# RWKV stage: bonus sums behind the next tile's dense products, decayed-key transposes one head pair later

## Chip, cores, metric

One core of one Trainium2 chip runs the whole program as a single launch. The metric is the device time of one execution in microseconds (us). The engines are named as in the profile: PE (TensorE, with PEld for its weight loads), DVE (VectorE), ACT (ScalarE), POOL (GpSimd), SP (SyncE, which here only issues DMAs).

## What is computed

The program is a chain of blocks on a 512x1024 activation: an RWKV-7 time mix with its MLP, a forgetting-attention layer with its MLP, a mixer (gated delta rule in both directions, and latent attention), and an expert-choice MLP. The change lies in the RWKV time mix only. What matters of the reference:

```python
r = xr @ wr
k = xk @ wk
v = xv @ wv
kk = split_heads(k * k_k)
kk = kk / jnp.maximum(jnp.sqrt(jnp.sum(kk * kk, axis=-1, keepdims=True)), L2_EPS)
k = k * (1.0 + (a - 1.0) * k_a)
y = wkv7_scan(rh, split_heads(decay), kh, vh, -kk, kk * ah)
bonus = jnp.sum((rh * kh * r_k), axis=-1, keepdims=True) * vh
```

There are 16 heads of 64 features. The scan over 512 tokens is done in 8 chunks of 64 tokens.

## The kernel before, in words

Activations are kept feature-major: a tile is 128 features (one pair of heads) by 512 tokens, and a 1024-wide tensor is 8 such tiles. The projections r, k and v are dense products in split precision. Each 128x1024 block of weights is loaded by SP (L179), rounded on ACT (`wh`, L181), and its remainder is taken on DVE (`wl`, L183). One output tile is then 24 matmuls on PE (L244 to L246, eight input tiles by three products). Two buffers each hold the raw, high and low weights, so the weights of a tile are made one tile ahead.

The stage of the change is the r projection. `dense_fm` with `use_r` runs over 8 output tiles p. After a tile's matmuls, `make_r` of the tile before runs. PE spreads a head's norm over the tile (`rB`, L303). DVE makes `kkn` from it (L673), then `kp` (L679), the product r·k·r_k (`prod`, L681) and the scan's left operand `ar` (L691 and L692, twice each). POOL makes `kka` (L675) and the right operand `bk` (L693, L694), and ACT makes the exponentials (L666, L668). Then `sum_bonus` (L656) sums `prod` over each head by four small matmuls into one PSUM bank that stays open for the whole stage.

`pairs(0, ...)` is a generator that is advanced by one head pair after each `make_r`, from the third tile on. For one pair it first issues two steps of `spare`, work for a later layer's modulation: each step is one 512 KB tile `mr` (DMA by SP, L328, four buffers) and two matmuls (L342). Then come eight matmuls `bk`x`ar` (L714) into two banks of their own (tag `f`, two buffers). DVE and ACT bring these to SBUF under masks (L723, L734 on DVE; L736 on ACT, then L737 on POOL). ACT or POOL (L746, L741) scales `bk` by the chunk's decay into `dg`, PE transposes `dg` in four pieces (L750), and ACT stores that as `Bh[p]` (L752), which only the scan reads.

After the r projection, `prepare(0)` inverts triangular blocks with a long chain on DVE (L786 to L805) while `pairs(1, ...)` does the second half of the tokens, and then the scan over chunks begins (L910).

Each engine executes its instructions in the order in which the build leaves them. That order is made by a scheduler from the traced program, and `tc.issue_after(x)` ties a traced instruction behind the instruction x on its engine. A wait on a semaphore holds everything that stands behind it on the same engine. Five PSUM banks (tag `b`) serve dense tiles, `rB`, the transposes and the bonus sum. A tile of the r projection is read from its bank until its last L692.

Of the kernel before, what the change touches and what calls it, by code (L numbers as in the profile page):

```python
# [12 lines left out]
AF = mybir.ActivationFunctionType  # L13
# [109 lines left out]
class K:  # L123
# [392 lines left out]
    def rwkv(self, x_dram, G, sh, gt, xT):  # L516
        nc, tc, A = self.nc, self.tc, self.A
# [127 lines left out]
        def use_r(p, pt):  # L645
            held.append((p, pt))
            if p:
                make_r(*held.pop(0))
            if p > 1:
                prep[0].send(None)  # L650

        prods = []

        def sum_bonus(p, prod):
            for tt in range(4):
                nc.tensor.matmul(pbon[:, tt * 16 + 2 * p:tt * 16 + 2 * p + 2], prod[:, tt * 128:tt * 128 + 128],  # L656
                                 self.cst("bo2"), start=(p == 0 and tt == 0), stop=(p == 7 and tt == 3),
                                 skip_group_check=True)

        def make_r(p, pt):  # L660
            rB = spr(p)
            cum, aa = CA[p]
            CA[p] = None
            W = self.wp.tile([128, 8, 65], F32, name=self.nm("W"), tag="w65")
            nc.gpsimd.memset(W[:, :, 0:1], 1.0)
            nc.scalar.activation(W[:, :, 1:65], cum.rearrange("p (c t) -> p c t", t=64), AF.Exp, scale=-C0)  # L666
            Wi = self.s()
            nc.scalar.activation(Wi, cum, AF.Exp, scale=C0)  # L668
            nc.gpsimd.tensor_copy(WCp[:, p, :], W[:, :, 64])
            nc.vector.tensor_copy(WCh[0:64, 2 * p, :], W[0:64, :, 64])  # L670
            nc.vector.tensor_copy(WCh[0:64, 2 * p + 1, :], W[64:128, :, 64])
            kkn = self.s()
            nc.vector.scalar_tensor_tensor(kkn, kT[p], self.col("rw_kk", p), rB, op0=OP.mult, op1=OP.mult)  # L673
            kka = self.s()
            nc.gpsimd.tensor_tensor(kka, kkn, aa, op=OP.mult)  # L675
            t = self.s()
            nc.scalar.activation(t, aa, AF.Identity, scale=self.col("rw_ka", p), bias=oka[:, p:p + 1])
            kp = self.s()
            nc.vector.tensor_tensor(kp, kT[p], t, op=OP.mult)  # L679
            prod = self.s()  # L680
            nc.vector.scalar_tensor_tensor(prod, pt, self.col("rw_rk", p), kp, op0=OP.mult, op1=OP.mult)  # L681
            prods.append((p, prod))
            if p:
                sum_bonus(*prods.pop(0))
            v3 = lambda x, hf: x[:, hf * 256:hf * 256 + 256].rearrange("p (c t) -> p c t", t=64)
            for hf in range(2):
                ar, bk = self.s(), self.s()
                AR[p][hf], BK[p][hf] = ar, bk
                a4, b4 = (z.rearrange("p (c t) -> p c t", t=128) for z in (ar, bk))
                cs = slice(hf * 4, hf * 4 + 4)  # L690
                nc.vector.scalar_tensor_tensor(a4[:, :, 0:64], v3(kkn, hf), -1.0, W[:, cs, 0:64], op0=OP.mult, op1=OP.mult)  # L691
                nc.vector.tensor_tensor(a4[:, :, 64:128], v3(pt, hf), W[:, cs, 1:65], op=OP.mult)  # L692
                nc.gpsimd.tensor_tensor(b4[:, :, 0:64], v3(kka, hf), v3(Wi, hf), op=OP.mult)  # L693
                nc.gpsimd.tensor_tensor(b4[:, :, 64:128], v3(kp, hf), v3(Wi, hf), op=OP.mult)  # L694

        gm = self.cst("gmask")
        idn = self.cst("ident")
        X, BKt, GB = [None, None], [None, None], [None, None]

        def pairs(hf, pool):  # L700

            GBh = GB[hf] = pool.tile([128, 32, 128], F32, name=self.nm("GB"), tag="gb", bufs=1)
            Xh = X[hf] = [None] * 16
            Bh = BKt[hf] = [None] * 8
            for p in range(8):
                g = p // 4
                ar, bk = AR[p][hf], BK[p][hf]
                self.spare(0 if hf else 2)
                pts = [self.bank("f"), self.bank("f")]
                for ci in range(4):  # L710
                    cs = slice(ci * 128, ci * 128 + 128)
                    for hd in range(2):
                        q = slice(hd * 64, hd * 64 + 64)
                        nc.tensor.matmul(pts[hd][:, cs], bk[q, cs], ar[q, cs], start=(ci == 0), stop=(ci == 3),  # L714
                                         skip_group_check=True)
                xo = self.s()
                nc.scalar.activation(xo[0:64], ar[64:128], AF.Copy)
                for hd in range(2):
                    u0 = ((2 * p + hd) % 8) * 4
                    v = pts[hd].rearrange("p (c t) -> p c t", t=128)  # L720
                    o = GBh[g * 64:g * 64 + 64, u0:u0 + 4, :]
                    if hf == 0:
                        nc.vector.tensor_tensor(o, v[0:64], gm[0:64].unsqueeze(1).to_broadcast([64, 4, 128]), op=OP.mult)  # L723
                    else:

                        nc.scalar.activation(o, v[0:64], AF.Copy)
                        nc.gpsimd.memset(o[32:64, :, 0:32], 0.0)
                        nc.gpsimd.tensor_tensor(o[:, :, 64:128], o[:, :, 64:128],
                                                gm[g * 64:g * 64 + 64, 64:128].unsqueeze(1).to_broadcast([64, 4, 64]), op=OP.mult)
                    dst = ar if hd == 0 else xo  # L730
                    d3 = dst[64:128].rearrange("p (c t) -> p c t", t=128)
                    mk = gm[64:128].unsqueeze(1).to_broadcast([64, 4, 128])
                    if hf == 0 and hd == 0:
                        nc.vector.tensor_tensor(d3, v[64:128], mk, op=OP.mult)  # L734
                    else:
                        nc.scalar.activation(d3, v[64:128], AF.Copy)  # L736
                        nc.gpsimd.tensor_tensor(d3, d3, mk, op=OP.mult)  # L737
                Xh[2 * p], Xh[2 * p + 1] = ar, xo
                dg = self.s()
                if hf == 0 and p % 2:  # L740
                    nc.gpsimd.tensor_tensor(dg.rearrange("p (c t) -> p c t", t=128), bk.rearrange("p (c t) -> p c t", t=128),  # L741
                                            WCp[:, p, hf * 4:hf * 4 + 4].unsqueeze(2).to_broadcast([128, 4, 128]), op=OP.mult)
                else:
                    for ci in range(4):
                        cs = slice(ci * 128, ci * 128 + 128)
                        nc.scalar.activation(dg[:, cs], bk[:, cs], AF.Copy, scale=WCp[:, p, hf * 4 + ci:hf * 4 + ci + 1])  # L746
                pt = self.ps()
                for ci in range(4):
                    cs = slice(ci * 128, ci * 128 + 128)
                    nc.tensor.transpose(pt[:, cs], dg[:, cs], idn)  # L750
                Bh[p] = self.s()
                nc.scalar.activation(Bh[p], pt, AF.Copy)  # L752
                yield

        prep = [pairs(0, gb0)]
        self.dense_fm(A["rw_wr"], xr, 0, D, use_r)
        make_r(*held.pop(0))
        prep[0].send(None)
        sum_bonus(*prods.pop(0))
# [6 lines left out]
        with tc.tile_pool(name="rwb", bufs=2, side="right", reuse_waits="tile") as bp:  # L766
# [116 lines left out]
            with self.behind(100000, slots=False):  # L883
                self.run(pairs(1, bp))
                next(pr1)
# [6 lines left out]
            for c in range(8):  # L892
                hf, ci = c // 4, c % 4
# [45 lines left out]
                mid = self.last_pe()  # L939
# [1483 lines left out]
```

## Time and profile before

| what | value |
|---|---|
| device time, three runs | 3038.48 us median (3029.11 to 3039.60) |
| profiled execution, its own time | 3032.97 us |
| span of the profiled execution | 3031.2 us |
| PE busy | 2777.4 us, 92% of the span |
| DVE, ACT, POOL busy | 1619.0, 1049.7 and 727.1 us |
| DMA | 502 MB, 166 GB/s over the span |

The profile's times count from the start of the span. Busy time of an engine is the union of its instructions. PEclk is the clock that TensorE was granted, as a share of full speed: 1.00 is 2.4 GHz, 0.50 is 1.2 GHz. In a timeline a row gives start, length, engine, line, output and inputs, a count, and in brackets the idle time before it with what ended it. A 32-bit matmul of this program can leave more than one record, so a count in the timeline can be a multiple of the number of instructions.

### The profile page before, as it was taken

The page shows a single profiled execution, that of the slowest core. Times are in us where ns is not written, and L with a number is a line of the kernel's source. Part 1 is how long each engine was busy: PE and PEld are TensorE (multiplying, and loading weights), DVE is VectorE, ACT ScalarE, POOL GpSimd, SP SyncE. Part 2 cuts the span into 40 slices and gives each one's busy share as a digit, 9 for nine tenths or more (in the row PEclk, how much of TensorE's full clock was granted, in tenths as well). Part 3 has the DMA queues.
Part 4 walks back from the last instruction along what each step waited for, and adds up shares of the span by engine and source line. Part 5 has one row for each costly group of instructions (what it writes and reads, how often), then busy time and mean ns, then how long its engine had stood idle before and what let it go on. Part 6 is the DMA issues. An engine that isn't in the chain of part 4 may idle for free. (4 is left out here: it accounts for less than half of the span.)

```text
span 3031.2 us, 38070 instructions
## 1 busy us (share of the span) xinstructions
PE 2777.4 (92%) x15046; PEld 1980.8 (65%) x15046; DVE 1619.0 (53%) x2449; ACT 1049.7 (35%) x1703; POOL 727.1 (24%) x563
## 2 busy tenths in 40 slices
PE   6997788999999999999999998898799997999997
PEld 1765466788877777778887776676677884444433
DVE  4565865456674447466645779647765542112112
ACT  2543533422234457442223452253334322110001
POOL 2444553211111034121113453135241121000000
PEclk8997767999999999999999999999999998999999
DMA  6332413346564321446531323242252358899998
GB/s 212 118 95 73 136 55 112 125 153 195 186 219 128 94 81 38 137 159 194 180 98 56 106 74 116 59 132 60 67 175 93 105 188 345 348 378 409 409 409 308
DMA packets 361010, 502.05 MB, mean 166 GB/s; under 512 B 24768, under 2 KB 236992, under 8 KB 360832
## 3 DMA queue, kind: packets, MB, share of 16 engines
q1 hardware_dynamic: 349600, 479.01, 46.5%
q10 hardware_dynamic: 11232, 20.62, 1.8%
q8 instruction: 118, 1.93, 0.3%
q14 instruction: 60, 0.49, 0.0%
HBM read 471.26 MB, written 26.21 MB: 164 GB/s over the span
## 5 line engine op out<-in xcount | busy, mean ns | idle before, releaser
L244 PE MATMUL psb<-s,wh 128*128 128x512 f32 x1384 | 546.1, 395 | 2.9 <-DVE s L977 2.2
L245 PE MATMUL psb<-s,wl 128*128 128x512 f32 x1384 | 543.3, 393 | 0.0
L246 PE MATMUL psb<-s,wh 128*128 128x512 f32 (+1 forms) x1320 | 515.0, 390 | 1.2 <-POOL s L481 0.6
L181 ACT ACTIVATE wh<-wr 128x1024 fp32r<-128x1024 f32 (+1 forms) x221 | 288.2, 1305 | 415.3 <-PE psb L246 266.1
L183 DVE TENSOR_TENSOR wl<-wr,wh 128x1024 fp32r<-128x1024 f32 (+1 forms) x145 | 260.1, 1795 | 261.3 <-ACT wh L181 261.0
L244 PEld LDWEIGHTS psb<-s,wh 128*128 128x128 f32 x1384 | 261.8, 189 | 71.7 <-issue 11.7
L245 PEld LDWEIGHTS psb<-s,wl 128*128 128x128 f32 x1384 | 261.4, 189 | 56.9 <-issue 2.6
L246 PEld LDWEIGHTS psb<-s,wh 128*128 128x128 f32 (+1 forms) x1320 | 247.4, 187 | 58.1 <-issue 2.9
L183 POOL TENSOR_TENSOR wl<-wr,wh 128x1024 fp32r<-128x1024 f32 (+1 forms) x76 | 185.8, 2447 | 397.6 <-ACT wh L181 378.8
L2123 PE MATMUL psb<-rg,s 128*64 128x512 f32 x1024 | 243.0, 598 | 5.3 <-DMA rg<-in_w_up_dram 3.8
L1312 PE MATMUL psf<-f,wh 128*128 128x512 f32 (+1 forms) x688 | 231.5, 410 | 11.0 <-ACT wh L181 10.9
L1008 POOL TENSOR_TENSOR s<-s 128x512 f32<-128x512 f32 x64 | 102.1, 1596 | 514.9 <-ACT s L1006 434.1
L2123 PEld LDWEIGHTS psb<-rg,s 128*64 128x64 f32 x1024 | 83.2, 137 | 142.3 <-issue 120.2
L1312 PEld LDWEIGHTS psf<-f,wh 128*128 128x128 f32 (+1 forms) x688 | 133.0, 194 | 43.1 <-ACT wh L181 12.3
L1312 PE MATMUL psf<-f,wl 128*128 128x512 f32 (+1 forms) x344 | 143.0, 416 | 15.5 <-POOL wl L183 15.4
L2151 PE MATMUL psb<-rg,s 128*64 128x512 f32 (+1 forms) x544 | 129.9, 621 | 0.0
L378 DVE SCALAR_TENSOR_TENSOR mt<-mr,crep,mt 128x512 f32<-128x512 f32 x168 | 126.5, 753 | 3.6
L201 ACT ACTIVATE s<-s 128x512 fp32r<-128x512 f32 x112 | 69.8, 625 | 136.3 <-POOL s L1008 73.1
L1015 DVE SCALAR_TENSOR_TENSOR s<-psb,aff,s 128x512 f32<-128x512 f32 x64 | 45.9, 751 | 129.5 <-PE psb L246 129.5
L1312 PE MATMUL psb<-f,wh 128*128 128x512 f32 (+1 forms) x336 | 107.8, 401 | 7.8 <-DVE f L479 5.9
L2151 PEld LDWEIGHTS psb<-rg,s 128*64 128x64 f32 x544 | 46.2, 148 | 74.2 <-issue 69.4
L1006 ACT ACTIVATE s<-psb 128x512 f32<-128x512 f32 x64 | 37.6, 588 | 164.0 <-PE psb L246 164.0
(565 smaller groups left out, 4946.4 us busy)
## 6 DMA issues: line engine op xcount, KB each, us to landing
rg<-in_w_gate_dram SPq DMA_DIRECT2D x64, 1024.0 KB
rg<-in_w_up_dram SPq DMA_DIRECT2D x64, 1024.0 KB
rg<-in_w_down_dram SPq DMA_DIRECT2D x64, 1024.0 KB
mr<-in_mod_w_dram SPq DMA_DIRECT2D x96, 512.0 KB
wr<-in_mlp_down_dram SPq DMA_DIRECT2D x32, 1024.0 KB
wr<-in_mlp_up_dram SPq DMA_DIRECT2D x31, 1024.0 KB
wr<-in_w_in_dram SPq DMA_DIRECT2D x54, 512.0 KB
mr<-in_w_mod_dram SPq DMA_DIRECT2D x40, 512.0 KB
```

The lines of the kernel that those rows point to most:

```text
L181: nc.scalar.activation(hi, raw, AF.Copy)
L183: (lo_eng or self.lo_eng or nc.vector).tensor_tensor(lo, raw, hi.bitcast(F32), op=OP.subtract)
L201: nc.scalar.activation(hi, src, AF.Copy)
L244: nc.tensor.matmul(pt[:mw], hi[k][:, j:j + mw], a, start=(k == 0), stop=False)
L245: nc.tensor.matmul(pt[:mw], lo[k][:, j:j + mw], a, start=False, stop=False)
L246: nc.tensor.matmul(pt[:mw], hi[k][:, j:j + mw], b, start=False, stop=(k == nk - 1))
L378: nc.vector.scalar_tensor_tensor(acc[:, hb], raw[:, d], c, acc[:, hb], op0=OP.mult, op1=OP.add)
L1008: nc.gpsimd.tensor_tensor(sq, r, r, op=OP.mult)
L1015: nc.vector.scalar_tensor_tensor(xT[m], pt, gt[:, m:m + 1], xT[m], op0=OP.mult, op1=OP.add)
L1312: nc.tensor.matmul(pt[:rows, :cols], x, y, start=(k == 0 and q == 0), stop=(k == nk - 1 and q == 2))
L2123: nc.tensor.matmul(B[n][q], XE[hp][k0 // 2][:, o:o + 64], w[e][:, k, n * 512:n * 512 + 512], start=(k0 + k == 0), stop=(k0 + k == 7), skip ...
L2151: last = nc.tensor.matmul(pt[q, :n], HT[(k + i) // 4][:, o:o + 64], w[e][i], start=(k + i == 0), stop=(k + i == 7), skip_group_check=True)
```

## The change

It does two things in the RWKV stage, and adds or removes no arithmetic.

- In `make_r(p)` the last PE instruction traced before (the end of the dense tile p+1, or what stands behind it) is noted as `mid`, and the bonus sums of tile p-1 are tied behind it. In the code before they were traced at the same place without that tie.
- In `pairs` the transposes of `dg` and their copy to `Bh` become a helper `turn`, called one head pair later; the last pair calls it twice. This holds for both halves of the tokens.

```diff
         def make_r(p, pt):
+            mid = self.last_pe()
             rB = spr(p)
@@
             prods.append((p, prod))
             if p:
-                sum_bonus(*prods.pop(0))
+                with tc.issue_after(mid):
+                    sum_bonus(*prods.pop(0))
@@
             Bh = BKt[hf] = [None] * 8
+            dgs = []
+
+            def turn(p, dg):
+                pt = self.ps()
+                for ci in range(4):
+                    cs = slice(ci * 128, ci * 128 + 128)
+                    nc.tensor.transpose(pt[:, cs], dg[:, cs], idn)
+                Bh[p] = self.s()
+                nc.scalar.activation(Bh[p], pt, AF.Copy)
+
             for p in range(8):
@@
-                pt = self.ps()
-                for ci in range(4):
-                    cs = slice(ci * 128, ci * 128 + 128)
-                    nc.tensor.transpose(pt[:, cs], dg[:, cs], idn)
-                Bh[p] = self.s()
-                nc.scalar.activation(Bh[p], pt, AF.Copy)
+                dgs.append((p, dg))
+                if p:
+                    turn(*dgs.pop(0))
+                if p == 7:
+                    turn(*dgs.pop(0))
                 yield
```

PE, between two dense tiles of the r projection, before. `psb_1433` is the tile just finished, `psb_1535` the next one, and `s_1476` the `prod` that DVE makes out of the spread norm in `psb_1458`:

```order
L246 MATMUL psb_1433<-xl_1195,wh_1428 128x512
L303 MATMUL psb_1458<-s_1210,s_1215 128x512
L714 MATMUL psf_1503<-s_1369,s_1370 128x128
L714 MATMUL psf_1504<-s_1369,s_1370 128x128
...
L656 MATMUL psb_1219<-C_62,s_1476 128x2 x4
L342 MATMUL psm_1598<-mr_1394,crep_80 32x512 x2
L342 MATMUL psm_1598<-mr_1494,crep_80 32x512 x2
L750 MATMUL psb_1522<-C,s_1520 128x128 x4
L244 MATMUL psb_1535<-s_819,wh_1530 128x512
```

The same place with the change, one tile on in the table of buffers. Lines behind the change are shifted, so L726 here is L714 of before and L713 is L750. `psb_1528` is finished and `psb_1633` comes next; `s_1469` is a `prod` made from the spread norm of the tile before, and the spread norm made here is `psb_1553`:

```order
L246 MATMUL psb_1528<-xl_1195,wh_1523 128x512
L303 MATMUL psb_1553<-s_1210,s_1215 128x512
L342 MATMUL psm_1390<-mr_1386,crep_80 32x512 x2
L342 MATMUL psm_1390<-mr_1388,crep_80 32x512 x2
L656 MATMUL psb_1219<-C_62,s_1469 128x2 x4
L726 MATMUL psf_1598<-s_1475,s_1476 128x128
L726 MATMUL psf_1599<-s_1475,s_1476 128x128
...
L713 MATMUL psb_1620<-C,s_1513 128x128 x4
L244 MATMUL psb_1633<-s_819,wh_1628 128x512
```

Before, the bonus sum between two tiles took a `prod` that starts from the spread norm two steps ahead of it on PE. With the change it takes the `prod` of one tile earlier, so a whole dense tile stands between the spread norm and the sum that depends on it.

ACT, the stretch that makes one tile's weights, before (L746 scales, L666 and L668 are the exponentials, L736 empties a bank of the pair products, L752 stores transposes):

```order
L746 ACTIVATE s_1415<-s_1303,WCp 128x128 x4
L666 ACTIVATE W_1562<-s_977 128x8x64
L736 ACTIVATE s_1408<-psf_1399 64x512
L752 ACTIVATE s_1425<-psb_1420 128x512
L668 ACTIVATE s_1463<-s_920 128x512
L181 ACTIVATE wh_1635<-wr_1634 128x1024
L677 ACTIVATE s_1472<-s_917,oka,P 128x512
```

The same stretch with the change (here L758 is L746 of before, L669 and L667 are L668 and L666, L748 is L736, L715 is L752, L678 is L677):

```order
L758 ACTIVATE s_1415<-s_1303,WCp 128x128 x4
L669 ACTIVATE s_1456<-s_920 128x512
L748 ACTIVATE s_1408<-psf_1399 64x512
L667 ACTIVATE W_1555<-s_977 128x8x64
L181 ACTIVATE wh_1628<-wr_1627 128x1024
L678 ACTIVATE s_1465<-s_917,oka,P 128x512
L729 ACTIVATE s_1506<-s_1369 64x512
L715 ACTIVATE s_1520<-psb_1515 128x512
```

The first store of transposes (`s_1425` before, `s_1520` with the change) has moved from ahead of the weights L181 to behind them. The copy of the pair product (`s_1408`) stays ahead of L181 in both.

## Rows read from the trace of the kernel before

**Rows 1.** The page: the span.
```profile
span 3031.2 us, 38070 instructions
```

**Rows 2.** Stretches: length, busy PE, PEld, DVE, ACT, POOL; PEclk; DMA share; GB/s.
```profile
187.00:199.00 12.00, 12.00 (x50) 8.87 (x49) 8.79 (x9) 6.39 (x8) 3.03 (x3) 1.00 0.16 45
...
211.00:223.00 12.00, 11.13 (x61) 8.12 (x61) 5.86 (x12) 3.77 (x6) 3.88 (x7) 0.86 0.60 206
223.00:235.00 12.00, 7.57 (x29) 5.30 (x30) 7.92 (x12) 3.30 (x6) 7.28 (x9) 0.72 0.37 117
...
303.00:388.00 85.00, 68.16 (x598) 43.55 (x590) 73.91 (x103) 48.94 (x99) 42.12 (x56) 0.68 0.38 122
```

**Rows 3.** Who waited for whom, PE, 185 to 320 us: total, times, longest.
```profile
PE psb L656 <- DVE s L681: 24.0, 7, 4.6
PE psb L750 <- POOL W L665: 1.6, 1, 1.6
```

**Rows 4.** Timeline of PE: the first step at full clock.
```profile
199.91 0.39 PE L244 MATMUL psb<-s,wh 128*128 128x512 f32 x1
...
205.52 0.39 PE L303 MATMUL psb<-s,s 128*128 128x512 f32 x1
205.74 0.95 PE L656 MATMUL psb<-C,s 128*128 128x2 f32 x8
206.62 1.16 PE L714 MATMUL psf<-s,s 64*128 64x128 f32 x16
207.71 1.06 PE L342 MATMUL psm<-mr,crep 128*32 128x512 f32 x8
```

**Rows 5.** Timeline of PE: rows of later steps and of the tail.
```profile
265.03 0.63 PE L245 MATMUL psb<-s,wl 128*128 128x512 f32 x1
265.46 0.63 PE L246 MATMUL psb<-xl,wh 128*128 128x512 f32 x1
...
286.86 0.40 PE L303 MATMUL psb<-s,s 128*128 128x512 f32 x1
...
291.57 1.16 PE L656 MATMUL psb<-C,s 128*128 128x2 f32 x8 [3.23 <-DVE s L681]
...
300.30 1.87 PE L656 MATMUL psb<-C,s 128*128 128x2 f32 x8 [3.21 <-DVE s L681]
...
325.23 0.66 PE L750 MATMUL psf<-C,s 128*128 128x128 f32 x4 [1.09 <-ACT s L736]
```

**Rows 6.** Timeline of DVE: one tile's work, and a row of an earlier tile.
```profile
222.66 2.33 DVE L183 TENSOR_TENSOR wl<-wr,wh 128x1024 fp32r<-128x1024 f32 x1 [0.16 <-ACT wh L181]
...
255.87 0.75 DVE L673 SCALAR_TENSOR_TENSOR s<-s,P,psb 128x512 f32<-128x512 f32 x1 [6.47 <-PE psb L303]
256.70 1.23 DVE L183 TENSOR_TENSOR wl<-wr,wh 128x1024 fp32r<-128x1024 f32 x1
257.85 1.75 DVE L679 TENSOR_TENSOR s<-s,s 128x512 f32<-128x512 f32 x1
...
260.12 0.73 DVE L681 SCALAR_TENSOR_TENSOR s<-psb,P,s 128x512 f32<-128x512 f32 x1
...
263.15 0.68 DVE L723 TENSOR_TENSOR GB<-psf,C 64x512 f32<-64x512 f32 x1
```

**Rows 7.** Timeline of ACT: the instructions of the ring that makes the weights.
```profile
255.62 1.06 ACT L181 ACTIVATE wh<-wr 128x1024 fp32r<-128x1024 f32 x1 [4.53 <-issue]
...
262.42 0.63 ACT L666 ACTIVATE W<-s 128x512 f32<-128x512 f32 x1 [4.39 <-DVE s L692]
...
265.40 0.62 ACT L668 ACTIVATE s<-s 128x512 f32<-128x512 f32 x1
266.04 0.59 ACT L736 ACTIVATE s<-psf 64x512 f32<-64x512 f32 x1
```

**Rows 8.** Timeline of POOL: the instruction beside DVE's first row above.
```profile
222.64 1.27 POOL L675 TENSOR_TENSOR s<-s,s 128x512 f32<-128x512 f32 x1 [5.53 <-ACT wh L181]
```

**Rows 9.** Timeline of PE in the first stage, where it waits for `mr` tiles.
```profile
23.02 1.05 PE L342 MATMUL psm<-mr,crep 128*32 128x512 f32 x4 [0.46 <-DMA mr<-in_mod_w_dram]
```

## The prediction

> **What bounds the kernel now.** I read first the page for the whole span [rows 1], then the stretches around the lines that the change touches, then the waits of PE there, and last the timelines of PE, DVE and ACT through single tiles.
>
> The stretches show a stage that is not at its limit [rows 2]. From 187 to 199 us, in the k projection, PE is busy 12.00 of 12 us at a granted clock of 1.00. In the r projection behind it PE is busy 7.57 of the 12 us from 223 on, and the mean clock is 0.72. No other engine is full there either: DVE 7.92, ACT 3.30, POOL 7.28. Something goes round in turns. The waits name it [rows 3]: between 185 and 320 us PE stands 24.0 us, in 7 waits, before the bonus sum L656, each time for `prod` (L681) on DVE. The chain is L303 on PE, then L673, L183, L679, L723, L681 on DVE, then L656 on PE, and behind L656 in PE's order stand the transposes and the next dense tile, which need nothing of it. In one tile DVE takes from 255.87 to 260.85 us to reach the end of L681 [rows 6], and PE has only the eight pair products to do meanwhile.
>
> The wait costs a second time. After it PE runs at the lower of its two clock levels (1.2 GHz of 1.2 and 2.4): the matmuls L245 and L246 at 265 us start 0.43 us apart [rows 5], where 24 of them at full clock took 205.52 - 199.91 = 5.61 us, 0.234 each [rows 4].
>
> **The change, part by part.** I count one step from one L303 to the next. The first L303 that matters is at 205.52 us [rows 4] and the sixth at 286.86 us [rows 5]: five steps in 81.3 us, 16.3 each.
>
> *PE's own work at full clock* [rows 4, 5]: L303 0.22 (205.52 to 205.74), the bonus sum 0.88 (to 206.62), the pair products 1.09 (to 207.71), two `mr` tiles about 1.0 (their row is 1.06 long and overlaps the next), four transposes 0.66, the dense tile 5.61. That is 9.46 us a step. With the change the first step holds neither `mr` tiles nor transposes: 7.8 us. One later step has two small matmuls more (L348), 0.3. So five steps take PE at least 7.8 + 4 x 9.46 + 0.3 = 45.9 us.
>
> *What is removed.* Of the 24.0 us of waits the last two, 3.23 and 3.21 [rows 5], lie behind the sixth L303; 17.6 lie in the five steps, and with POOL's 1.6 [rows 3] it is 19.2. The same five steps hold about 48.6 us of PE work at full clock before (five times 8.46, six groups of two `mr` tiles, 0.3). The rest, 81.3 - 48.6 - 19.2 = 13.5 us, is what the lower clock and the interleaving of transposes took. If PE no longer waits, both go: the waits, and the clock, since PE at 12.00 of 12 us kept a clock of 1.00 [rows 2].
>
> *What is moved.* The bonus sum now stands one dense tile behind its `prod`: that is 9.46 us after the L303 that starts a chain of 5.0 us, so it should be met. The transposes of pair p-1 stand where those of pair p stood, on a `dg` made one step earlier; nothing in the stage reads `Bh`, so L752 has no waiter but its own bank. One group of two `mr` tiles comes out of the first step, one out of a later one. They run in the tail behind the sixth L303, 1.0 us each at full clock and about 1.8 at the lower (0.43 over 0.234). The two waits of 3.2 us in that tail cover them. If that cover were gone they would cost up to 3.6 us. SP's loads of `mr` follow these matmuls, because a buffer comes free only with them.
>
> *What is late next.* Two chains then run beside PE. DVE's tile goes from 255.87 to 263.83 us, L673 to the last L723 [rows 6], 8.0 us; with L303's 0.39 us [rows 4] ahead of it, 8.4 a step. The second is a ring. L183 on DVE waits for L181 on ACT, which in ACT's order stands behind L736, which waits for the last L723 of the DVE tile before. L183's start to L723's end is 7.1 us [rows 6]; L736 0.59, one or both exponentials at 0.62, and L181 1.06 make 2.3 to 2.9 [rows 7]. The ring takes 9.4 to 10.0 us, against PE's 9.46. No row shows two in-order chains of nearly one length leaning on each other, so I bound it. From below it is PE's 9.46. From above every DVE instruction that POOL can hold up is held up. The row at 222.66 shows L183 at 2.33 us beside L675 on POOL, which had started first and ran 1.27 [rows 8]; the row at 256.70 shows it at 1.23. With 1.27 added to L183 and to each of the two L691 (L679, 1.75 long, has its share in that tile [rows 6]), DVE's tile is 8.0 + 3.8 = 11.8 and the step about 12.2 with L303. I take 10.2, nearer the lower end, because the measured ring of 9.4 to 10.0 already has one such hold in it.
>
> The Trainium skill, on the page "SBUF — State Buffer", section "Who interferes with whom", says that a VectorE instruction with two inputs in SBUF and a GpSimd instruction that reads SBUF exclude each other for the whole instruction. This case's rows agree with it (L183 at 2.33 beside POOL, 1.23 otherwise). It speaks against the change: the denser the steps, the less of POOL's work finds DVE idle. Read strictly it favours the upper bound: a step of 12.2 and a gain of 24 us, where the sum below takes 10.2 and 32.
>
> *The sum.* 7.8 + 4 x 10.2 + 0.3 = 48.9 us in place of 81.3: 32 us less. Behind the sixth L303 I count nothing. The tail is again a chain through DVE with PE waiting. The stretch behind it is DVE's: 73.91 of 85 us from 303 to 388 [rows 2]. There the transposes of the second half move by one pair beside a long DVE chain, and their last store stands ahead of the last copies that the scan waits for; I put that at 0, between -2 and +3 (one transposition group and one store, 0.66 and 0.6, at either clock, each once or twice). Everything later starts earlier by what is gained.
>
> The profiled execution took 2 us more than its span, 3032.97, which is 5.5 below the median of the three runs and 3.9 above the lowest. As the level of no change I take 3035, about the mean of these four. The forecast is 3035 - 32 = **3003 us**.
>
> **The rivals.**
>
> 1. *DVE and POOL become the bound.* Steps of 12.2 instead of 10.2. For it: DVE 7.92 and POOL 7.28 us busy in a stretch of 12 us [rows 2] while the steps are 16.3 long, and the two rows of L183 [rows 6]. Against: ACT and DVE still idle in every tile before. The time would be 7.8 + 4 x 12.2 + 0.3 = 56.9, a gain of 24: 3011.
> 2. *The gain is given back later.* The stretch of 85 us behind the stage, or a stage whose loads are not ready earlier, takes back most of it. For it: `mr` tiles, transposes and scan preparation are all in that stretch. Against: it is paced by a DVE chain that reads nothing moved. If half to all is lost: 3019 to 3035.
> 3. *Slower: PE waits for `mr` tiles.* The `mr` matmuls now stand ahead of the bonus sum, the pair products, the transposes and the dense tile, so a late DMA holds all of them, and a step needs two tiles. It decides where a step passes (81.3 - 7.8) / 4 = 18.4 us, 9.2 us a tile; at 12 us a tile it would be 7.8 + 96 = 104 us, 3058. Against it: in the first stage, where PE waits for them, a tile lands about every 1.05 + 0.46 = 1.5 us [rows 9], and the DMA engines are 0.60 busy at most here [rows 2].
> 4. *The change does not do what it says.* The order of instructions shows that it does: between the dense tiles only sums of the tile before are left. What is left of it is that the wait reappears at L303, which needs a bank that DVE's last L692 frees; that is rival 1 with another releaser.
>
> **How the numbers follow.** A measurement of this kernel can tell about 0.5% from no change, 15 us: faster means below 3023. The forecast has 0.62, rival 1 has 0.21, rival 2 has 0.12 (a quarter of it still below 3023), rival 3 has 0.05. That gives 0.86; I take 0.84 for faster, 0.11 for the same, 0.05 for slower, since the unseen part of rival 2 is the one that I can't price from rows. The range runs from PE's own limit with a little of the tail (3035 - 35.4 - 5 = 2994, rounded) past rival 1 into the first part of rival 2: 2994 to 3022.
>
> **What would show it.** Right: L656 no longer waits for L681 in the first five steps; L303 comes every 9.5 to 11 us; the granted clock in the r projection is above 0.95; the first L786 comes some 32 us earlier, and the scan's first L910 by as much. Rival 1: L303 waits for DVE, L183 stands at 2.3 in most tiles. Rival 2: the r projection is shorter, but the distance from the first L786 to the first L910 grew. Rival 3: PE's waits name `in_mod_w`. I am wrong if PE waits over 10 us in the five steps, or if the steps keep 16 us.

## Result, and the profile after

The change takes 2995.99 us (median of 4 runs, 2993.68 to 2999.24) against 3037.69 us before (4 runs, 3029.11 to 3039.6): a ratio of 0.9869, 95% interval 0.9848 to 0.9890. The forecast was 3003 us, the range 2994 to 3022, so it was 7 us too long and the time lies near the range's lower end. The profiled execution took 2999.24 us, 33.7 less than the profiled one of before (3032.97).

More lines of the changed kernel and their lines before: L682 was L681, L735 and L746 were L723 and L734, L753 was L741, L797 was L786, L803 was L792, L921 was L910. The page, the change:

```profile
span 2997.4 us, 38061 instructions
```

Against [rows 1] the span lost 33.8 us. Stretches of the change (length; busy PE, PEld, DVE, ACT, POOL; granted clock; DMA share; GB/s):

```profile
205.00:253.00 48.00, 48.00 (x296) 35.28 (x299) 42.24 (x73) 26.21 (x46) 36.88 (x45) 1.00 0.40 121
211.00:223.00 12.00, 12.00 (x64) 7.89 (x63) 11.11 (x19) 5.37 (x8) 9.15 (x12) 1.00 0.50 136
223.00:235.00 12.00, 12.00 (x79) 8.35 (x77) 9.32 (x18) 7.58 (x14) 9.13 (x12) 1.00 0.27 87
265.00:350.00 85.00, 69.16 (x602) 43.05 (x603) 75.08 (x107) 50.38 (x101) 43.36 (x57) 0.66 0.42 134
```

Where PE was busy 11.13 and 7.57 of 12 us at a clock of 0.86 and 0.72 [rows 2], it is now busy all the time at 1.00. The stretch behind, 303 to 388 us before, is 38 us earlier and as it was: DVE 75.08 of 85 against 73.91. Who waited for whom, PE, 185 to 320 us:

```profile
PE psm L342 <- issue: 2.5, 1, 2.5
PE psf L713 <- ACT s L748: 2.0, 2, 1.3
PE psf L726 <- ACT s L748: 1.9, 3, 0.7
PE psb L713 <- POOL s L753: 1.7, 2, 1.1
PE psb L656 <- DVE s L682: 1.4, 1, 1.4
...
```

The bonus sums waited 24.0 us in 7 waits [rows 3]; what is left is one of 1.4, in the tail behind the sixth L303. Between 205 and 253 us PE has no wait at all; all rows above lie behind that, in the tail and in the preparation of the scan. Timeline of PE, two pieces: the second of the five steps, and the third:

```profile
212.18 0.39 PE L303 MATMUL psb<-s,s 128*128 128x512 f32 x1
212.50 1.05 PE L342 MATMUL psm<-mr,crep 128*32 128x512 f32 x4
213.48 0.38 PE L656 MATMUL psb<-C,s 128*128 128x2 f32 x2
213.79 1.05 PE L342 MATMUL psm<-mr,crep 128*32 128x512 f32 x2
214.77 0.38 PE L656 MATMUL psb<-C,s 128*128 128x2 f32 x2
215.08 1.04 PE L342 MATMUL psm<-mr,crep 128*32 128x512 f32 x2
...
223.72 0.40 PE L303 MATMUL psb<-s,s 128*128 128x512 f32 x1
224.04 1.06 PE L342 MATMUL psm<-mr,crep 128*32 128x512 f32 x8
225.04 1.05 PE L656 MATMUL psb<-C,s 128*128 128x2 f32 x8
226.02 1.16 PE L726 MATMUL psf<-s,s 64*128 64x128 f32 x16
227.11 0.66 PE L713 MATMUL psb<-C,s 128*128 128x128 f32 x4
...
233.14 0.40 PE L303 MATMUL psb<-s,s 128*128 128x512 f32 x1
```

L303 starts at 204.28, 212.18, 223.72, 233.14, 242.57 and 252.54 us: steps of 7.90, 11.54, 9.42, 9.43 and 9.97, together 48.3 us where before took 81.3. From there the gain is carried: the sixth L303 is 34.3 us earlier, the first L797 34.8 (269.0 against 303.8), the scan's first L921 37.6 (345.1 against 382.7), its last 34.0 (460.0 against 494.0), and behind the scan the gain of single instructions moves between about 31 and 36 us and is 33.8 at the end.

### The profile page after: what moved, and what is told of

It reads as the page before. It is cut to its first block, busy times and chain, and to the rows that moved or that the text cites. A ratio compares the mean times of both kernels' runs of the same rounds, so it can differ in the third digit from the quotient of the medians.

```text
span 2997.4 us, 38061 instructions
## 1 busy us (share of the span) xinstructions
PE 2766.3 (92%) x15046; PEld 1971.0 (66%) x15046; DVE 1615.5 (54%) x2449; ACT 1049.1 (35%) x1703; POOL 726.7 (24%) x563
## 5 line engine op out<-in xcount | busy, mean ns | idle before, releaser
L181 ACT ACTIVATE wh<-wr 128x1024 fp32r<-128x1024 f32 (+1 forms) x221 | 288.1, 1304 | 397.9 <-PE psb L246 263.9
L183 DVE TENSOR_TENSOR wl<-wr,wh 128x1024 fp32r<-128x1024 f32 (+1 forms) x145 | 260.7, 1799 | 262.8 <-ACT wh L181 260.4
L244 PEld LDWEIGHTS psb<-s,wh 128*128 128x128 f32 x1384 | 259.4, 187 | 70.7 <-issue 11.4
L183 POOL TENSOR_TENSOR wl<-wr,wh 128x1024 fp32r<-128x1024 f32 (+1 forms) x76 | 185.5, 2443 | 401.4 <-ACT wh L181 386.1
L1323 PE MATMUL psf<-f,wl 128*128 128x512 f32 (+1 forms) x344 | 142.7, 415 | 16.6 <-POOL wl L183 16.5
L1017 ACT ACTIVATE s<-psb 128x512 f32<-128x512 f32 x64 | 37.6, 588 | 164.0 <-PE psb L246 164.0
```

What stands on the lines that cost most here:

```text
L181: nc.scalar.activation(hi, raw, AF.Copy)
L183: (lo_eng or self.lo_eng or nc.vector).tensor_tensor(lo, raw, hi.bitcast(F32), op=OP.subtract)
L244: nc.tensor.matmul(pt[:mw], hi[k][:, j:j + mw], a, start=(k == 0), stop=False)
L1323: nc.tensor.matmul(pt[:rows, :cols], x, y, start=(k == 0 and q == 0), stop=(k == nk - 1 and q == 2))
```

## The experiments

Theory: before, PE stood in each step for a product just started, and paid twice, for the wait and for the lower clock behind it. Rivals: one half of the change does all; the clock has nothing to do with it; the transposes were the wait.

| kernel | five steps, us | PE's waits in them, us | median, us (runs) | ratio to before, 95% interval |
|---|---|---|---|---|
| before | 81.3 | 19.1 | 3037.69 (4) | 1 |
| the change | 48.3 | 0 | 2995.99 (4) | 0.9869, 0.9848 to 0.9890 |
| e1_tie_only | 63.3 | 11.4 | 3018.15 (4) | 0.9945, 0.9930 to 0.9960 |
| e2_late_transposes_only | 48.3 | 0 | 2996.08 (4) | 0.9872, 0.9854 to 0.9890 |
| e6_tie_and_scaling_on_act | 50.6 | 3.3 | 3004.09 (4) | 0.9890, 0.9875 to 0.9905 |
| e3a_wait_forced | 71.9 | 16.7 | 3039.91 (10) | 1.0009, 0.9999 to 1.0018 |
| e4_no_spare_groups_in_steps | 44.3 | 1.8 | 2999.13 (4) | 0.9878, 0.9858 to 0.9898 |

Steps are read from L303 to L303 (L306 in e3a), beginning with the second. Each ratio is to runs of before made beside that kernel, with medians of 3035.85 to 3037.69 us.

**One half at a time.** e1: the kernel before with the tie alone.

```diff
+            mid = self.last_pe()
...
-                sum_bonus(*prods.pop(0))
+                with tc.issue_after(mid):
+                    sum_bonus(*prods.pop(0))
```

> The tie of the bonus sums alone, on the kernel before; the transposes stay with their own pair, behind its products. Theory (the 33 us are the waits of the bonus sums for the product of L681, and the lower clock that followed them): the bonus sums wait no more, but the transposes now stand right behind the products of their own pair, and their scaled keys come behind ACT's copies of those products, so a part of the wait returns there: 1.5 to 3.5 us a step at the transposes, the five steps take 55 to 68 us instead of 81.3 (before) and 48.3 (the change), total 3003 to 3018. Rival 1 (the tie alone does it, the place of the transposes is free): no wait, five steps 48 to 50, total 2994 to 3000. Rival 2 (only the later transposes count): the wait goes whole to the transposes, five steps 78 or more, total 3030 or more.

Its steps are 9.59, 17.65, 9.23, 17.35 and 9.47 us. Timeline of PE, e1, in the second step (L752 are the transposes):

```profile
217.07 1.06 PE L342 MATMUL psm<-mr,crep 128*32 128x512 f32 x8
224.32 1.12 PE L752 MATMUL psb<-C,s 128*128 128x128 f32 x4 [6.18 <-POOL W L666]
```

and of POOL, e1, at the same time:

```profile
217.02 1.29 POOL L676 TENSOR_TENSOR s<-s,s 128x512 f32<-128x512 f32 x1
218.39 1.59 POOL L695 TENSOR_TENSOR s<-s,s 128x256 f32<-128x256 f32 x1
220.60 0.73 POOL L696 TENSOR_TENSOR s<-s,s 128x256 f32<-128x256 f32 x1 [0.63 <-DVE s L680]
221.29 0.94 POOL L695 TENSOR_TENSOR s<-s,s 128x256 f32<-128x256 f32 x1
222.19 0.90 POOL L696 TENSOR_TENSOR s<-s,s 128x256 f32<-128x256 f32 x1
223.05 1.22 POOL L743 TENSOR_TENSOR s<-s,WCp 128x512 f32<-128x512 f32 x1
224.21 0.11 POOL L666 MEMSET W<- 128x8 f32 x1
```

The bonus sums wait no more, and three of the five steps are as short as the change's. In the others PE stands before the transposes for the scaled keys of L743. The profile names the tiny L666, which starts when L743 ends; L743 itself waits for nothing but its queue, five multiplies of the next pair's tiles (with 0.63 us in which POOL in turn waits for L680 on DVE). Only odd pairs are scaled on POOL. So the size was as expected (55 to 68 us; the total a touch above its range), but the wait is POOL's order, not ACT's copies. e6 takes that apart: e1 with every pair scaled by ACT.

```diff
-                if hf == 0 and p % 2:
+                if False:
```

> The tie alone (e1_tie_only), and the scaled keys of the odd pairs made by ACT as those of the even ones, instead of by POOL; the transposes stay with their own pair. In e1_tie_only the steps alternate, 9.6, 17.7, 9.2, 17.4 us, and PE's waits stand at the transposes of odd pairs alone. Theory (the later transposes of the change are there for POOL, whose multiply of L743 stands behind four multiplies of the next pair's decayed tiles): the odd steps fall to 9.2 to 11 us, the five steps take 47 to 52 us, total 2994 to 3003, as the whole change. Rival 1 (ACT becomes late in turn, four scalings of each pair behind its copies): waits of 1 to 3 us at the transposes of every pair, steps of 10.5 to 13, total 3003 to 3016. Rival 2 (the wait was for the decayed tiles themselves, L695 and L696, not for POOL's queue): odd steps stay over 15 us, total 3012 or more.

Steps of 9.60, 10.59, 10.34, 10.34 and 9.76 us: the 17 us steps are gone though L743's input is the same, so it was POOL's queue. ACT is late in turn, as rival 1 has it, but by 1.0 to 1.3 us at a time (3.3 in the five steps). The median is some 8 us above the change's and just above the theory's range (3003); 2.3 of them are in the five steps, and from the sixth L303 to the start of the scan's preparation (L797 of the change) it takes 20.4 us instead of 16.5, with one wait of 3.7 us of PE for DVE there. The profiled executions differ by only 2.2 us. e2 is the other half: the change without the tie.

```diff
-                with tc.issue_after(mid):
-                    sum_bonus(*prods.pop(0))
+                sum_bonus(*prods.pop(0))
```

> The later transposes alone, without the tie. The instructions of the five engines then stand in the same order as in the whole change, so it is the same program again: theory: five steps 48 to 49 us, no wait at the bonus sums, total 2994 to 3001, which would make the tie of no effect in this place. Rival (the tie changes something besides the order, such as a semaphore wait): the bonus sums wait again, five steps over 55 us, total over 3005. For the later stretch: if the 6 us that the profile of the change loses in the second half of the scan come from the clock's phase in that one execution, this run shows another amount (0 to 8 us); if they belong to the program, it shows 5 to 7 again.

48.3 us and 2996.08: the same program in effect, since all five engines have their instructions in the same order with and without the tie. With the transposes a pair later, the scheduler leaves the bonus sums behind the next dense tile without being told. In the text the change has two parts; in this place the late transposes alone make both moves.

**The wait and the clock.** e3a forces a wait into the changed kernel: the pair's products are made in its own step, its bonus sums are asked for at once, and the next dense tile is tied behind them.

```diff
-            held.append((p, pt))
-            if p:
-                make_r(*held.pop(0))
+            make_r(p, pt)
             if p > 1:
                 prep[0].send(None)
+            sum_bonus(*prods.pop(0))
+            if p < 7:
+                self.behind_this = self.last_pe()
```

> The changed kernel with a wait forced into each step: the products of a head pair are made at once in its own step, its bonus sums are asked for at once, and the next dense tile is tied behind them, so that PE waits in each step for a product that has just been started. Theory (such a wait costs twice: its own length and the lower clock behind it): PE waits 3 to 6 us a step, the granted clock of the stretch falls from 1.00 to 0.70 to 0.85, and a step takes 2 to 3 us more than 9.6 plus the wait, 15 to 18 us; total 3035 to 3065 over its seven such steps. Rival (the wait costs its length alone): clock 1.00 for the busy stretches, steps of 12.5 to 15.5 us, each equal to 9.4 to 9.6 plus its wait; total 3018 to 3038.

The time of before is back: 3039.91 us, with 16.7 us of waits in five steps and 71.9 us in place of 48.3. The waits came out at the lower end of what was expected (3.3 us a step) and the steps below it, 14.4 us and not 15 to 18; the mean clock over them is 0.83. Steps of 14.4 us lie in the rival's 12.5 to 15.5 too, though 3.3 us of wait on 9.5 make 12.8. Waits and clock still stand in one kernel, so a pair parts them. Both halves are e3a with L342 out of the steps; e3d fills the wait with matmuls whose result nobody reads.

```diff
+            if p < 7:
+                with tc.issue_after(self.last_pe()):
+                    for i in range(20):
+                        nc.tensor.matmul(pbon[:, 128:512], xr[p][0][:, 0:128], xr[p][0][:, 0:384],
+                                         start=(p == 0 and i == 0), stop=False, skip_group_check=True)
             sum_bonus(*prods.pop(0))
```

> The kernel with the forced wait (e3a_wait_forced), its two groups of L342 taken out of each step as in e4_no_spare_groups_in_steps, so that nothing but the wait stands between the transposes and the bonus sums. It is the one half of a pair; the other fills the same wait with work. In e3a_wait_forced a step took 14.4 us on average with 2.9 us of wait; without the 1.0 us of groups the wait should be 3.5 to 4.5 us and a step 13.5 to 15.0 us, with dense rows 0.43 us apart behind each wait in place of 0.23. Total 3030 to 3048.

> The same kernel with 20 matmuls of 128x384 (about 0.17 us each by the dense rows, 3.5 us in all) in front of the bonus sums of steps one to seven; they write a part of the bank that nobody reads, so PE works through the wait, and the product is ready no sooner. Theory (a wait costs its length and then a lower clock): the granted clock stays at 1.00 in the steps, the dense rows stay 0.23 us apart, and a step takes 12.0 to 12.8 us, 1.5 to 2.5 us less than in the unfilled half, though PE does more; total 10 to 18 us below the unfilled half. Rival (the wait costs its length alone): the steps of both halves differ by less than 0.5 us, or the filled ones are longer; total within 4 us of the unfilled half or above it.

Unfilled (e3c) 3050.23 us (5 runs; ratio 1.0048, 1.0032 to 1.0064), filled (e3d) 3036.23 (10 runs; 1.0004, 0.9994 to 1.0014): 14.0 us less with 140 matmuls more. The same step of each; timeline of PE, e3c:

```profile
246.80 0.39 PE L306 MATMUL psb<-s,s 128*128 128x512 f32 x1
...
252.85 1.87 PE L660 MATMUL psb<-C,s 128*128 128x2 f32 x8 [3.99 <-DVE s L685]
254.58 0.77 PE L246 MATMUL psb<-s,wh 128*128 128x512 f32 x1
255.15 0.63 PE L247 MATMUL psb<-s,wl 128*128 128x512 f32 x1
255.58 0.63 PE L248 MATMUL psb<-xl,wh 128*128 128x512 f32 x1
...
261.84 0.39 PE L306 MATMUL psb<-s,s 128*128 128x512 f32 x1
```

and e3d (L655 are the fillers, L664 the bonus sums):

```profile
237.53 0.40 PE L306 MATMUL psb<-s,s 128*128 128x512 f32 x1
...
239.36 3.72 PE L655 MATMUL psb<-s 128*128 128x384 f32 x20
...
243.61 1.05 PE L664 MATMUL psb<-C,s 128*128 128x2 f32 x8 [0.53 <-DVE s L689]
244.52 0.48 PE L246 MATMUL psb<-s,wh 128*128 128x512 f32 x1
244.84 0.40 PE L247 MATMUL psb<-s,wl 128*128 128x512 f32 x1
245.07 0.40 PE L248 MATMUL psb<-xl,wh 128*128 128x512 f32 x1
...
250.22 0.39 PE L306 MATMUL psb<-s,s 128*128 128x512 f32 x1
```

From L306 to the bonus sums both take the same (6.05 and 6.08 us). Behind them the unfilled step needs 1.73 us for the sums and 7.26 for the dense tile, the filled one 0.91 and 5.70: the first dense rows behind the wait, up to 258.11, start 0.43 us apart, the lower of the two clock levels (1.2 GHz of 1.2 and 2.4), and 0.23 in the filled step. Over the last four filled steps, stretches, first e3c:

```profile
246.80:302.00 55.20, 41.63 (x213) 33.18 (x212) 31.48 (x49) 20.82 (x35) 29.41 (x32) 0.85 0.04 10
```

then e3d:

```profile
237.50:286.40 48.90, 48.31 (x293) 41.24 (x292) 31.66 (x49) 20.87 (x35) 29.64 (x32) 1.00 0.04 12
```

DVE, ACT and POOL do the same work; the clock is 0.85 in the one, 1.00 in the other, and a step 13.8 and 12.2 us. The lower clock is a price of its own, and it comes from PE standing still, not from the wait's cause: shown. For a mean wait of 3.4 us (13.6 in four) filling gained 1.6 us a step. The price itself is nearer 2.0, since PE is busy 41.63 us in the one and, without some 14.7 of fillers, 33.6 in the other. The step shown is one of the dearer ones, 15.04 against 12.69.

**What bounds a step now.** e4 takes L342 out of the five steps and puts the groups behind them.

```diff
-                self.spare(0 if hf else 2)
+                self.spare(2 if not hf and p > 5 else 0)
...
-                    self.spare(16)
+                    self.spare(28)
```

> The changed kernel with the two groups of L342 (four matmuls, 1.0 us) taken out of each of the five steps and put into the stretch behind (prepare asks for 28 instead of 16), where PE waits for DVE. Theory (a step of the change is bound by PE's own work): steps of 8.3 to 8.6 us instead of 9.4 to 10.0, the five steps 42 to 44 instead of 48.3, 4 to 6 us gained, total 2989 to 2994 if the stretch behind hides the groups. Rival 1 (the ring through DVE, ACT and the exponentials, which was estimated at 9.4 to 10.0 us, bounds a step as closely): steps stay at 9.2 or more with PE idle 0.5 to 1 us a step, under 1.5 us gained, 2994 to 3000. Rival 2 (the groups delay the stretch behind, by transfers or by PE's queue): steps shorter but the first L803 not earlier, total 2996 to 3006.

Steps of 7.89, 9.54, 8.25, 8.79 and 9.81 us: 4.0 us less in all, out of some 5.9 us of L342, so PE's own work bounds the change's steps. But PE now waits 1.8 us in them, for DVE and ACT: the ring is about as close as that. The 4.0 us are lost in the stretch behind, as rival 2 has it (the first L803 at 279.9 us, 279.8 in the change), in a place that it did not name. Who waited for whom, DVE, 268 to 345 us, the change:

```profile
DVE mt L345 <- PE psm L342: 3.2, 2, 2.8
```

and e4:

```profile
DVE mt L345 <- PE psm L342: 6.4, 2, 4.3
```

Each four groups end in a transposition on DVE (L345), and there DVE is the engine with little time to spare (67.57 of the change's 76.06 us). From the first L797 to the scan's first product it takes 83.9 us instead of 76.1. The longer waits before L345 are 3.2 us of these 7.8, and one more L345 is 0.7; where the rest goes was not taken apart. No gain in total (2999.13).

**The lesson tried on the scan.** The change has one long wait more, 6.75 us between L821 and L828 of the scan's second half, with the lower clock behind it. e5 fills it; c0 is the change again, measured beside it.

```diff
+                    if hf and ub == 0:
+                        self.keep_pe(12)
...
+    def keep_pe(self, n):
+        pt, rep = self.bank("m"), list(self.crep.values())[0]
+        with self.tc.issue_after(self.last_pe()):
+            for _ in range(n):
+                self.nc.tensor.matmul(pt[:, 0:256], self.cst("ident"), rep[:, 0:8, :].rearrange("p a b -> p (a b)"), start=True, stop=True)
```

> The change itself once more, beside the kernel with the filled wait in the preparation of the second half: 2993 to 3000 us by the runs so far.

> The change with 12 matmuls of 128x256 (ident by the replicated conditioning, 0.52 us each by half the row of L865, 6.3 us in all) into a bank that nobody reads, in the one long wait that the change's profile has in the scan: 6.75 us between L821 and L828 of the second half, from 397.6 to 404.4 us. Theory (what follows a wait runs at the lower clock because of the wait): the rows from 404 to 430 us, of which the profile of the change shows most at the lower level, run at full clock; by those rows (L828 1.91 to about 1.1, L921 0.91 and 3.04 to 0.5 and 1.7, L953 1.53 to 1.14, L946 and L953 1.97 to 1.14, L865 2.07 to 1.05, L921 3.68 to 2.08) that is up to 7 us in the one execution; the distance from the first to the last L921 shrinks from 112 to 115 us to 104 to 110, and the total falls by 3 to 8 us against the change in the same call. Rival 1 (the clock falls again later in the scan wherever it had been, as its phase moves): the distance shrinks by less than 2 us, total within 2 us. Rival 2 (the fillers delay L828, or the chain there is ACT's and DVE's): the wait's end moves back, total 1 to 6 us longer.

c0 2997.22 us (4 runs; ratio 0.9867, 0.9852 to 0.9882), e5 2998.91 (4 runs; 0.9873, 0.9856 to 0.9889): no gain. From the first to the last product of the scan (L921, L923 in e5) it takes 115.0 us in e5, not the 104 to 110 expected, and 111.7 in c0. Timeline of PE, e5 (L2311 are the fillers, L821 and L830 the products around the wait):

```profile
403.48 5.45 PE L2311 MATMUL psm<-crep,C 128*128 128x256 f32 x24
...
410.61 1.10 PE L830 MATMUL psb<-GB,W 32*32 32x32 f32 x57 [0.37 <-ACT W L826]
411.61 1.74 PE L821 MATMUL psb<-TT,GB 32*32 32x32 f32 x59
416.68 0.31 PE L830 MATMUL psb<-GB,W 32*32 32x32 f32 x2 [3.33 <-ACT W L826]
...
417.76 1.91 PE L830 MATMUL psb<-GB,W 32*32 32x32 f32 x62
```

The filled wait did keep the clock: 57 records of L830 take 1.10 us behind it, and 62 take 1.91 further down. But with the fillers in place the scheduler also put the second half of L821 behind those L830, ACT got it later, and a wait of 3.33 us (1.43 in c0) opened there, with the lower clock behind it. So one filled wait brought nothing here, with the next right behind it; the changed order has its part in that, and whether filling them all would pay was not tried.

## Why the prediction was right, and where its sizes were off

*The path.* Right in kind and in size: the waits for L681 were the path, and with them went the lower clock. The sum had 48.9 us for the five steps; they took 48.3, and the gain there is 33.1 where the forecast had 32.4 (81.3 - 48.9). The waits are gone as said, the clock is 1.00 where over 0.95 was asked.

*Its terms, less so.* First step 7.8, measured 7.90. Later steps were put at 10.2, between PE's 9.46 and 12.2; three took 9.42, 9.43 and 9.97, PE's own work and little more. The ring of 9.4 to 10.0 us is not the floor that it was taken for: e4 has steps of 8.25 and 8.79. The one step above the term, 11.54 us, is none of the causes that I had: its four L342 (two records each) stand as two, one and one with bonus sums between them, and each of the three pieces holds PE for 1.0 us (212.50 to 213.48, 213.79 to 214.77, and again) where four adjacent ones take 1.0 in all (224.04 to 225.04). So the sum came right by luck, by an overestimate in three steps and an omission in one.

*Rival 1, the port.* It is true of single instructions. Timeline of DVE, the change:

```profile
216.14 2.19 DVE L183 TENSOR_TENSOR wl<-wr,wh 128x1024 fp32r<-128x1024 f32 x1
...
225.00 1.30 DVE L183 TENSOR_TENSOR wl<-wr,wh 128x1024 fp32r<-128x1024 f32 x1
```

and of POOL:

```profile
217.19 1.19 POOL L670 COPY WCp<-W 128x8 f32<-128x8 f32 x1
222.98 0.19 POOL L670 COPY WCp<-W 128x8 f32<-128x8 f32 x1
```

A copy of 128x8 takes POOL 1.19 us beside L183 and 0.19 without it. That agrees with the Trainium skill, "SBUF — State Buffer", section "Who interferes with whom". The prediction's L183 of 1.23 us at 256.70 [rows 6] was not free of POOL, as it was read: L675 started 0.06 us behind it and took 2.29 us, where it had taken 1.27 [rows 8], so there it was POOL that was held. But PE waits for neither, so steps of 12.2 us did not come: DVE's 42.24 busy us of 48 hold its share of such waiting, and still leave room.

*Rival 2, given back later.* It did not happen. From the first L797 to the scan's first L921 it takes 76.1 us where it took 78.9. In the change's own profile the scan is longer (first to last L921 114.9 us against 111.3), but e2 and c0, the same order of instructions, have 112.2 and 111.7. L921 of the second half's second chunk, timeline of PE, the change:

```profile
425.21 3.68 PE L921 MATMUL psb<-s,s 128*64 128x64 f32 x64
```

and c0:

```profile
425.67 2.08 PE L921 MATMUL psb<-s,s 128*64 128x64 f32 x64
```

One program, one place, the lower level in one execution and full clock in the other: this part is not the change's. Rival 3 (PE waiting for `mr` tiles) has no row in the five steps, and rival 4 no row at L303.

*The step that was off.* "Behind the sixth L303 I count nothing." From the second L303 to the scan's first product the three executions of this order gained 36.4 (the change), 38.0 (e2) and 35.6 us (c0), 33.1 of it in the five steps: the tail and the preparation gave 2.5 to 4.9 us more, outside the -2 to +3 on the better side. Up to the first L797 it is 0.5, 1.4 and 1.2 of that (in the same order), the rest is the preparation; which of the moved instructions gave it no run tells apart. The other part is the level of no change: 3035 was taken, about the mean of four times; the medians of before beside the change and the experiments are 3035.85 to 3038.02. The 41.7 us between the medians is more than any pair of profiles shows (33.8, 32.7 and 36.6 us in the spans); the profiled execution of before is one of its shorter ones, and where its longer ones lose their 5 us no profile here shows. By the medians, 41.7 is more than the range's lower end allowed (35.4 and 5 of the tail), and the time lies inside only because the level was set 2.7 us too low: that part is luck.

## What to carry to other kernels

Ask of an in-order engine's wait what it costs behind itself: here a wait of 3 to 4 us of PE took about 2 us more through the clock, and 14.0 of the 33.1 us won in the steps stood in no row of waits. A product needed by a small sum should be one tile of independent work old when the sum is issued; look then which queue becomes the next to be late (POOL's, in e1), since curing one wait alone left 11.4 of 19.1 us of waiting, in a new place. And before taking work out of a full stretch, follow what it brings along: e4's matmuls made DVE wait longer for its transpositions' input in the stretch where DVE had little time to spare.

## What was not expected of the hardware

Throwaway matmuls made a kernel with forced waits 14.0 us faster. And four L342, each on its own 32 columns of the array, take 1.0 us together when adjacent (row 224.04 of the change), and one of them alone between bonus sums takes as long (rows 213.79 and 215.08). The Trainium skill, "TensorEngine Tiling (Array Packing)", section "Key Properties", says that tiles work in parallel and that a change of the tiling mode drains the engine. These rows agree with the first; whether a drain has a part in the 1.0 us they do not show.
